# Sums of weight blocks by accumulating DMAs instead of VectorE subtractions, in a hybrid decoder block on one Trainium2 core

## The chip, the cores and the metric

The program runs on one core of one Trainium2 chip. The metric is the device time of one execution in microseconds (us); the figure used is the median of several executions. Engines are called as in the profile: PE (TensorE matmul), PEld (its weight loads), DVE (VectorE), ACT (ScalarE), POOL (GpSimd), SP (SyncE, which here only issues DMAs).

## The reference

One decoder block on x (256 tokens, 1024 channels). A normalised input goes through one input projection w_in; a gated linear recurrence (HGRN2) and a block attention (MoBA) work on parts of it; both branch outputs are projected, each gated by a sigmoid, summed, and projected again; a SwiGLU network follows. What matters here is the gate of the first branch, gates[:, :, 0, :], and where it is used:

```python
h = rmsnorm(x, attn_norm_g[l])
proj = h @ w_in[l]
hq, hf, hi, hg, aq, ak, av, gl = jnp.split(proj, IN_SPLITS, axis=-1)
y_hg = hgrn2_mix(hq, hf, hi, hg, lb_all[l], hg_out_norm_g[l]) @ w_branch_hg[l]
...
y_at = att.transpose(0, 2, 1, 3).reshape(B, S, AT_WIDTH) @ w_branch_attn[l]
gates = jax.nn.sigmoid(gl.reshape(B, S, N_BRANCH, D))
merged = gates[:, :, 0, :] * y_hg + gates[:, :, 1, :] * y_at
```

## The kernel before

Weights are float32 and go through PE as two float32r parts: ACT writes the rounded part (`whi`, line 55), DVE the rest (`wlo`, line 56), and each product is three matmuls (hi by hi, lo by hi, hi by lo). Weights come in pieces of 128x2048 floats (1 MB), loaded by SP into a ring of three buffers `wraw`; `whi` and `wlo` have three buffers each. Every engine works its instructions off in a fixed order.

The first branch's gate is a product of 256 tokens x 1024 channels with 1024 columns of w_in that start at column 7168 (`g0`). It isn't computed straight. Tokens are cut in two halves (0 to 127, 128 to 255), channels in two halves, columns in two halves: a 2x2 by 2x2 block product, done with seven block products instead of eight (a scheme of the Strassen kind). Write Bij for the weight block with channel half i and column half j, each 512x512 and 1 MB. `quarter(i, j, tag)` loads one block (tiles W11, W12, W22, W21 in the code). The scheme needs sums and differences of token blocks (made in `token_sums`, lines 585 to 599, tiles C, Ch, Cl) and of weight blocks. The weight tile W11 takes four contents in turn, and after each of them `halves(W11)` splits it (ACT line 55, DVE line 56) for one block product:

- content 1: B11, product b1 with plain tokens;
- content 2: a difference of B12 and B11 (line 676), product b3 with token sum 0;
- content 3: B22 minus content 2 (line 683), product b2 with token sum 1;
- content 4, held in W21: B21 minus content 3 (line 702), last product b2 with plain tokens.

W12 becomes B22 minus B12 (line 684), for token sum 2. These four subtractions are DVE instructions on 128x2048 floats.

The block products (`product`, line 620, 12 matmuls each) alternate on PE with half column blocks of the attention branch's projection (`step`, lines 657 to 659, 24 matmuls each, weights w_at). The order of PE is: b1 of content 1; transposes `turn` (line 442) of the recurrence's output; step; b3 of content 2; step; b2 of content 3; b1 with B21; step; b2 with W12; step; b3 with B22; b2 of content 4; then the projection w_hg. `then` and `issue_after` pin this order. `put` (lines 446 to 457) turns the transposes into the split tiles oT. In the traces the four W tiles are all called W.

Of the kernel before, what the change touches and what calls it, by code (L numbers as in the profile page):

```python
# [7 lines left out]
F32 = mybir.dt.float32  # L8
F32R = mybir.dt.float32r
U32 = mybir.dt.uint32  # L10
AF = mybir.ActivationFunctionType
OP = mybir.AluOpType
AX = mybir.AxisListType

P = 128
S = 256
# [11 lines left out]
def tile_hgrn2_moba_block(ctx: ExitStack, tc: tile.TileContext, xm, xT, vecs, table, onehot,  # L28
                          w_in, w_hg, w_at, w_out, w_gate, w_up, w_down, out):
    nc = tc.nc  # L30
    const = ctx.enter_context(tc.tile_pool(name="const", bufs=1))
# [6 lines left out]
    def pw(name="pw"):  # L38
        return psum.tile([P, 512], F32, name=name, tag="pw", bufs=4)
# [4 lines left out]
    def pa(name="pa"):  # L44
        return psum.tile([P, 512], F32, name=name, tag="pa", bufs=2)
# [8 lines left out]
    def split(src, hi, lo):  # L54
        high = nc.scalar.copy(hi, src)  # L55
        return high, nc.vector.tensor_sub(lo, src, hi.bitcast(F32))  # L56

    halved = []
# [95 lines left out]
    for kt in range(KT):  # L154
        i = kt % 2
# [17 lines left out]
        else:  # L173
# [3 lines left out]
                                       op0=OP.mult, op1=OP.subtract)  # L177
        nc.scalar.copy(wh[:, i, 512:D], raw[:, i, 512:D])  # L178
        for hs in (slice(0, 512), slice(512, D)):
            low = nc.vector.tensor_sub(wl[:, i, hs], raw[:, i, hs], wh[:, i, hs].bitcast(F32))  # L180
# [15 lines left out]
    for j in range(7):  # L196
        c = 1 << j
# [9 lines left out]
    def rinv(dst, ss, n):  # L207
        nc.vector.tensor_scalar(dst, ss, 1.0 / n, EPS, op0=OP.mult, op1=OP.add)
        nc.scalar.activation(dst, dst, AF.Sqrt)
        nc.vector.reciprocal(dst, dst)  # L210
# [35 lines left out]
        nc.scalar.activation(junk, xtok[:, tb, :], AF.Square, accum_out=ss[:, tb:tb + 1])  # L246
    rx = const.tile([P, 2], F32, name="rx")
    rinv(rx, ss, D)
    def put_tok(dst, ps, half):
        for tb in range(2):  # L250
            nc.scalar.mul(dst[:, tb, half * 512:(half + 1) * 512], ps[tb], rx[:, tb:tb + 1])

    put_tok(V, V0, 0)
    put_tok(V, V1, 1)
    R = const.tile([P, S], F32, name="R")
    spread(R, rx)
# [7 lines left out]
    for half in range(2):  # L264
        ps = F0 if half == 0 else feat_block(w_in, 1024 + half * 512, XT, cut=2 - half)
        for j in range(2):
# [8 lines left out]
            for i in range(2):  # L275
                hh = slice(h + i, h + i + 1)
                nc.vector.tensor_scalar(Fg[:, :, h + i, :], Fg[:, :, h + i, :], lc[:, hh], lb[:, hh],
                                        op0=OP.mult, op1=OP.add)
# [151 lines left out]
    def hgrn_gate(o, ro, sg, banks):  # L430
        for tb in range(2):
            for h in range(H):
                hs = slice(h * P, (h + 1) * P)
                nc.vector.scalar_tensor_tensor(o[:, tb, hs], o[:, tb, hs], ro[:, tb, h:h + 1], sg[:, tb, hs],
                                               op0=OP.mult, op1=OP.mult)
        oT = [big.tile([P, 4, 2, S], F32R, name=f"oT{i}", tag=("T3", "T4")[i]) for i in range(2)]
        for g in range(4):
            bank = banks[g]
            for i in range(2):
                for tb in range(2):  # L440
                    h = 2 * g + i
                    last = nc.tensor.transpose(bank[:, i * S + tb * P:i * S + (tb + 1) * P],
                                               o[:, tb, h * P:(h + 1) * P], ident)

        def put(high, low):
            for g in range(4):
                q = 2 * g % 4
                with tc.issue_after(high.ins):
                    nc.scalar.mul(oT[g // 2][:, q:q + 2, 0, :], banks[g].rearrange("p (h t) -> p h t", h=2), og)
            for g in range(4):  # L450
                q = 2 * g % 4
                with tc.issue_after(low.ins):
                    nc.vector.scalar_tensor_tensor(oT[g // 2][:, q:q + 2, 1, :],
                                                   banks[g].rearrange("p (h t) -> p h t", h=2), og,
                                                   oT[g // 2][:, q:q + 2, 0, :].bitcast(F32),
                                                   op0=OP.mult, op1=OP.subtract)

        return oT, put, last


    def qk_block(tok, sq, c0, half, bank=pw):
        put_tok(tok, tok_block(w_in, c0 + half * 512, XT, bank=bank), half)
        for tb in range(2):
            for h in range(half * 4, half * 4 + 4):
                jk = small.tile([P, P], F32, name="jk")
                nc.scalar.activation(jk, tok[:, tb, h * P:(h + 1) * P], AF.Square, accum_out=sq[:, tb, h:h + 1])
# [119 lines left out]
    def token_sums():  # L586
        F = big.tile([P, 2, 4, S], F32, name="F", tag="T1")
        C = big.tile([P, 4, 4, P], F32, name="C", tag="T3")
        hi = big.tile([P, 4, 4, P], F32R, name="Ch", tag="T5")
        lo = [big.tile([P, 2, 4, P], F32R, name=f"Cl{i}", tag=("T13", "T15")[i]) for i in range(2)]  # L590
        for i in range(2):
            nc.vector.tensor_add(F[:, i], XT[i][:, :, 0, :].bitcast(F32), XT[i][:, :, 1, :].bitcast(F32))
        nc.vector.tensor_add(C[:, 0], F[:, 0, :, P:S], F[:, 1, :, P:S])
        nc.vector.tensor_sub(C[:, 1], C[:, 0], F[:, 0, :, 0:P])
        nc.vector.tensor_sub(C[:, 2], F[:, 0, :, 0:P], F[:, 0, :, P:S])
        nc.vector.tensor_sub(C[:, 3], F[:, 1, :, 0:P], C[:, 1])
        for i in range(2):
            split(C[:, 2 * i:2 * i + 2], hi[:, 2 * i:2 * i + 2], lo[i])
        return [hi[:, c] for c in range(4)], [lo[c // 2][:, c % 2] for c in range(4)]


    g0 = 7168

    def quarter(i, j, tag):
        t = big.tile([P, 4, 512], F32, name=f"W{i}{j}", tag=tag)
        nc.sync.dma_start(t, w_in[i * 512:(i + 1) * 512, g0 + j * 512:g0 + (j + 1) * 512]
                          .rearrange("(k p) c -> p k c", p=P))
        return t

    def halves(raw):  # L610
        hi = wp.tile([P, 4, 512], F32R, name="whi")
        lo = wp.tile([P, 4, 512], F32R, name="wlo")
        halved.append(split(raw, hi, lo))
        return hi, lo
# [9 lines left out]
    def tokens(i, j):  # L624
        return lambda kt, m: XT[j][:, kt, m, i * P:(i + 1) * P]

    def summed(c):
        return lambda kt, m: sums[m][c][:, kt, :]
# [3 lines left out]
    A01 = hgrn_cross()  # L632
    o, ro = hgrn_out(A01)
    sums = token_sums()
    W11 = quarter(0, 0, "T9")
    W12 = quarter(0, 1, "T1")
    branch_gate(1, 1)
    turn_a, b1, turn_h, b3 = pa("turn"), pa("b1"), ph("turn"), ph("b3")
    product(b1, tokens(0, 0), halves(W11), True)
    oT, put_oT, at = hgrn_gate(o, ro, sg, (turn_a, turn_h, pw("turn"), pw("turn")))  # L640

    def then(f, *args):
        with tc.issue_after(at.ins):
            return f(*args)
# [3 lines left out]
    def at_block(half):  # L648
        ps = [pw(), pw()]
        steps = chunks(w_at, half * 512, 512, (4, 4))  # L650

        def step():
            for _ in range(4):
                kt, wh, wl = next(steps)
                for tb in range(2):
                    ts = slice(tb * P, (tb + 1) * P)
                    nc.tensor.matmul(ps[tb], part(aT, kt, 0)[:, ts], wh, start=(kt == 0), stop=False)  # L657
                    nc.tensor.matmul(ps[tb], part(aT, kt, 0)[:, ts], wl, start=False, stop=False)  # L658
                    mm = nc.tensor.matmul(ps[tb], part(aT, kt, 1)[:, ts], wh, start=False, stop=(kt == KT - 1))  # L659
            return mm  # L660

        def out():
            hs = slice(half * 512, (half + 1) * 512)
            for tb in range(2):
                nc.vector.tensor_mul(G[1][:, tb, hs], G[1][:, tb, hs], ps[tb])

        return step, out

    def gq(i, j):
        return G[0][:, i, j * 512:(j + 1) * 512]  # L670

    def sigmoid(i, j, src):
        nc.scalar.activation(gq(i, j), src, AF.Sigmoid, scale=rx[:, i:i + 1])

    nc.scalar.copy(gq(1, 0), b1)
    nc.vector.tensor_sub(W11, W12, W11)
    step0, out0 = at_block(0)
    at = then(step0)
    at = then(product, b3, summed(0), halves(W11), True)
    W22 = quarter(1, 1, "T8")  # L680
    at = then(step0)
    with tc.issue_after(halved[-1][1].ins):
        nc.vector.tensor_sub(W11, W22, W11)
        low = nc.vector.tensor_sub(W12, W22, W12)
    put_oT(halved[-1][0], low)
    b2 = pa("b2")
    at = then(product, b2, summed(1), halves(W11), True)
    W21 = quarter(1, 0, "T2")
    at = then(product, b1, tokens(0, 1), halves(W21), False)
    sigmoid(0, 0, b1)  # L690
    step1, out1 = at_block(1)
    at = then(step1)
# [3 lines left out]
    at = then(product, b2, summed(2), halves(W12), False)  # L696
# [1 line left out]
    nc.vector.tensor_add(gq(1, 1), gq(1, 1), b3)  # L698
    sigmoid(1, 1, gq(1, 1))
    at = then(step1)  # L700
    with tc.issue_after(halved[-1][1].ins):
        nc.vector.tensor_sub(W21, W21, W11)
    out1()
    at = then(product, b3, summed(3), halves(W22), False)
    nc.vector.tensor_add(gq(0, 1), gq(0, 1), b3)
    sigmoid(0, 1, gq(0, 1))
    at = then(product, b2, tokens(1, 1), halves(W21), False)
    nc.vector.tensor_add(gq(1, 0), b2, gq(1, 0))
    sigmoid(1, 0, gq(1, 0))

# [148 lines left out]
```

## Time and profile before

| | before |
|---|---|
| median of 3 runs | 497.64 us (497.56 to 498.19) |
| profiled execution | 498.32 us, its span 496.3 us, so 2.0 us lie around the span |
| PE busy in the span | 490.4 us |
| DVE busy | 362.5 us |
| ACT busy | 290.7 us |
| POOL busy | 20.3 us |
| granted clock of PE | 1.000 |

The span runs from the first to the last instruction. Busy time counts instructions at work, not waits. An engine that is busy nearly all of the span sets the time; what the others do matters where it makes that engine wait.

### The profile page before, as it was taken

How to read it: one execution, taken by the hardware profiler on the slowest of the kernel's cores; microseconds unless marked ns; L12 is line 12 of the kernel's file. 1: busy time of each engine (PE TensorE's matmuls, PEld its weight loads, DVE VectorE, ACT ScalarE, POOL GpSimd, SP SyncE). 2: the span in 40 equal slices, each digit the busy share in tenths (PEclk: the TensorE clock that was granted, in tenths of full speed). 3: DMA queues.
4: the chain of work that ended last, by engine and by line, in shares of the span. 5: the costliest groups of instructions: out<-in, count | busy, mean ns of one | idle time of the engine just before them, and what ended most of it. 6: DMA issues, size and time to landing. Idle time of an engine off the chain costs nothing.

```text
span 496.3 us, 6659 instructions
## 1 busy us (share of the span) xinstructions
PE 490.4 (99%) x2664; PEld 414.6 (84%) x2664; DVE 362.5 (73%) x414; ACT 290.7 (59%) x410; POOL 20.3 (4%) x43
## 2 busy tenths in 40 slices
PE   8999999999999999999999999999999999999997
PEld 6888888888888888988888888888888888888885
DVE  5769999697679948499987767777636746566373
ACT  5877646777748964874564445764545435444350
POOL 0900220000000000000000000000000000000000
PEclk9999999999999999999999999999999999999999
DMA  8977685624544454327338555555565555643522
GB/s 272 395 269 255 222 255 183 233 85 154 188 169 167 145 198 147 109 81 257 129 127 280 183 183 186 182 173 170 174 221 191 177 173 193 219 136 108 188 86 86
DMA packets 43518, 91.20 MB, mean 184 GB/s; under 512 B 1976, under 2 KB 5336, under 8 KB 43488
## 3 DMA queue, kind: packets, MB, share of 16 engines
q1 hardware_dynamic: 42608, 88.12, 52.0%
q0 software_dynamic: 736, 2.65, 1.7%
q8 instruction: 21, 0.34, 0.3%
q14 instruction: 9, 0.07, 0.0%
q10 hardware_dynamic: 144, 0.02, 0.0%
HBM read 89.70 MB, written 1.07 MB: 183 GB/s over the span
## 4 chain that ended last, share of the span: by engine, by line
PE 98%; DMA 1%; SPq 0%; ACT 0%; DVE 0%; issue 0%
PE pw L101 23%; PE pw L100 10%; PE pw L83 10%; PE pw L84 10%; PE pw L85 10%; PE pw L151 4%; PE acc L782 4%; PE acc L781 4%; PE acc L780 4%; PE b L620 4%; PE pw L658 1%; PE pw L657 1%; PE pw L659 1%; PE pw L103 1%; PE ph L369 1%; DMA wraw<-w_in 1%
## 5 line engine op out<-in xcount | busy, mean ns | idle before, releaser
L56 DVE TENSOR_TENSOR wlo<-wraw,whi 128x2048 fp32r<-128x2048 f32 (+1 forms) x77 | 167.6, 2179 | 87.3 <-ACT whi L55 86.8
L55 ACT CAST whi<-wraw 128x2048 fp32r<-128x2048 f32 (+1 forms) x77 | 140.2, 1823 | 98.0 <-PE pw L85 30.9
L101 PE MATMUL pw<-x2T,whi 128*128 128x512 f32 x352 | 121.9, 398 | 0.0
L100 PE MATMUL pw<-x2T,wlo 128*128 128x256 f32 x308 | 86.6, 281 | 0.0
L101 PEld LDWEIGHTS pw<-x2T,whi 128*128 128x128 f32 x352 | 63.6, 188 | 12.5
L100 PEld LDWEIGHTS pw<-x2T,wlo 128*128 128x128 f32 x308 | 58.3, 189 | 1.8
L83 PE MATMUL pw<-whi,XT 128*128 128x512 f32 x144 | 56.9, 395 | 0.0
L84 PE MATMUL pw<-wlo,XT 128*128 128x512 f32 x144 | 56.2, 391 | 0.0
L85 PE MATMUL pw<-whi,XT 128*128 128x512 f32 x144 | 56.2, 391 | 0.0
L101 PE MATMUL pw<-XT,whi 128*128 128x512 f32 x128 | 44.5, 398 | 0.0
L780 PE MATMUL acc<-whi,hT 128*128 128x512 f32 x86 | 33.5, 390 | 0.0
L782 PE MATMUL acc<-whi,hT 128*128 128x512 f32 x86 | 33.5, 390 | 0.0
L781 PE MATMUL acc<-wlo,hT 128*128 128x512 f32 x86 | 33.5, 390 | 0.0
L85 PEld LDWEIGHTS pw<-whi,XT 128*128 128x128 f32 x144 | 27.0, 188 | 5.6
L83 PEld LDWEIGHTS pw<-whi,XT 128*128 128x128 f32 x144 | 27.1, 188 | 5.6
L84 PEld LDWEIGHTS pw<-wlo,XT 128*128 128x128 f32 x144 | 27.1, 188 | 5.5
L100 PE MATMUL pw<-XT,wlo 128*128 128x256 f32 x112 | 31.5, 281 | 0.0
L101 PEld LDWEIGHTS pw<-XT,whi 128*128 128x128 f32 x128 | 23.2, 188 | 4.5
L100 PEld LDWEIGHTS pw<-XT,wlo 128*128 128x128 f32 x112 | 21.2, 189 | 0.7
L781 PEld LDWEIGHTS acc<-wlo,hT 128*128 128x128 f32 x86 | 16.2, 188 | 3.4
L782 PEld LDWEIGHTS acc<-whi,hT 128*128 128x128 f32 x86 | 16.2, 188 | 3.4
L151 PE MATMUL pw<-whi,XT 128*128 128x512 f32 x64 | 17.7, 393 | 1.2 <-ACT whi L178 1.2
(290 smaller groups left out, 821.6 us busy)
## 6 DMA issues: line engine op xcount, KB each, us to landing
wraw<-w_in SPq DMA_DIRECT2D x26, 1024.0 KB, 5.0
wraw<-w_down SPq DMA_DIRECT2D x11, 1024.0 KB, 4.7
wraw<-w_gate SPq DMA_DIRECT2D x10, 1024.0 KB, 5.0
wraw<-w_up SPq DMA_DIRECT2D x10, 1024.0 KB, 5.0
wraw<-w_in SPq DMA_DIRECT2D x10, 512.0 KB, 7.8
W<-w_in SPq DMA_DIRECT2D x4, 1024.0 KB, 5.0
wraw<-w_at SPq DMA_DIRECT2D x4, 1024.0 KB, 4.9
wraw<-w_hg SPq DMA_DIRECT2D x4, 1024.0 KB, 5.7
```

What stands on the lines that cost most here:

```text
L55: high = nc.scalar.copy(hi, src)
L56: return high, nc.vector.tensor_sub(lo, src, hi.bitcast(F32))
L83: nc.tensor.matmul(ps[tb], part(act, kt, 0)[:, ts], wh, start=(kt == 0), stop=False)
L84: nc.tensor.matmul(ps[tb], part(act, kt, 0)[:, ts], wl, start=False, stop=False)
L85: nc.tensor.matmul(ps[tb], part(act, kt, 1)[:, ts], wh, start=False, stop=(kt == KT - 1))
L100: nc.tensor.matmul(ps[ct][:, 0:S], lo[:, i, cs], part(act, kt, 0), start=False, stop=False)
L101: nc.tensor.matmul(ps[ct], hi[:, i, cs], both, start=(kt == 0), stop=(kt == KT - 1))
L151: nc.tensor.matmul(ps[tb], part(XT, kt, am)[:, tb * P:(tb + 1) * P], w[:, i, hs], start=(kt == 0 and am == 0 and w is wh), stop=(kt == KT ...
L620: mm = nc.tensor.matmul(bank, act(kt, m), h[:, kt, :], start=(first and kt == 0 and m == 0 and h is hi), stop=(kt == 3 and m == 1), skip_g ...
L780: nc.tensor.matmul(acc[tb][half], act[:, j, 0, ts], hi[:, i, cs], start=st, stop=False)
L781: nc.tensor.matmul(acc[tb][half], act[:, j, 0, ts], lo[:, i, cs], start=False, stop=False)
L782: nc.tensor.matmul(acc[tb][half], act[:, j, 1, ts], hi[:, i, cs], start=False, stop=en)
```

## The change

The weight sums become plain sums: W11 holds in turn B11, B11+B12, B11+B12+B22 and B11+B12+B22+B21, and W12 holds B12+B22. Each addition is a DMA that POOL issues and that adds a block from HBM into the tile (`accum_op=OP.add`). The signs move into the token sums (two subtractions become `scalar_tensor_tensor` with a factor of -1) and into two sigmoids, which take the scale rn = -rx for columns of half 1. The four DVE subtractions go. B12, B22 and B21 are still loaded into tiles of their own, so the adds read 4 MB more from HBM.

```diff
+    rn = const.tile([P, 2], F32, name="rn")
+    nc.vector.tensor_scalar_mul(rn, rx, -1.0)
...
-        nc.vector.tensor_add(C[:, 0], F[:, 0, :, P:S], F[:, 1, :, P:S])
-        nc.vector.tensor_sub(C[:, 1], C[:, 0], F[:, 0, :, 0:P])
+        nc.vector.tensor_sub(C[:, 0], F[:, 1, :, P:S], F[:, 0, :, P:S])
+        nc.vector.scalar_tensor_tensor(C[:, 1], C[:, 0], -1.0, F[:, 0, :, 0:P], op0=OP.mult, op1=OP.subtract)
...
-        nc.vector.tensor_sub(C[:, 3], F[:, 1, :, 0:P], C[:, 1])
+        nc.vector.scalar_tensor_tensor(C[:, 3], F[:, 1, :, 0:P], -1.0, C[:, 1], op0=OP.mult, op1=OP.subtract)
...
+    def block(i, j):
+        return w_in[i * 512:(i + 1) * 512, g0 + j * 512:g0 + (j + 1) * 512].rearrange("(k p) c -> p k c", p=P)
...
+    def add_quarter(t, i, j):
+        nc.gpsimd.dma_start(t, block(i, j), accum_op=OP.add)
...
-        nc.scalar.activation(gq(i, j), src, AF.Sigmoid, scale=rx[:, i:i + 1])
+        nc.scalar.activation(gq(i, j), src, AF.Sigmoid, scale=(rx, rn)[j][:, i:i + 1])
...
-    nc.vector.tensor_sub(W11, W12, W11)
+    add_quarter(W11, 0, 1)
...
-    with tc.issue_after(halved[-1][1].ins):
-        nc.vector.tensor_sub(W11, W22, W11)
-        low = nc.vector.tensor_sub(W12, W22, W12)
-    put_oT(halved[-1][0], low)
+    add_quarter(W11, 1, 1)
+    add_quarter(W12, 1, 1)
+    put_oT(*halved[-1])
...
     W21 = quarter(1, 0, "T2")
+    add_quarter(W11, 1, 0)
...
-    with tc.issue_after(halved[-1][1].ins):
-        nc.vector.tensor_sub(W21, W21, W11)
...
-    at = then(product, b2, tokens(1, 1), halves(W21), False)
+    at = then(product, b2, tokens(1, 1), halves(W11), False)
```

How the instructions stand now is shown at two places. The first is POOL's queue at its end. Before, it holds one load of x (the tokens again, for the residual sum) behind two copies of the attention bias:

```order
L312 COPY B_577<-Bx 128x1024 [waits DMASW1_49,PE_49]
L312 COPY B_578<-Bx 128x8x128 [waits DMASW3_49]
L714 DMA x_2274<-xm 128x2x1024 [waits DMAHW4_49,DMAHW5_49,DMAHW1_49,DMAHW7_49,DMAHW0_49,DVE_49]
```

Of the change, W_1898 is W11 and W_1900 is W12:

```order
L315 COPY B_579<-Bx 128x1024 [waits DMASW1_49,PE_49]
L315 COPY B_580<-Bx 128x8x128 [waits DMASW3_49]
L616 DMA W_1900<-w_in 128x4x512 [waits DMAHW1_49,DMAHW4_49,DMAHW0_49,DMAHW5_49,DVE_49,DMAHW7_49,PE_49,Activation_49]
L616 DMA W_1898<-w_in 128x4x512 [waits DVE_49]
L616 DMA W_1898<-w_in 128x4x512 [waits DMASW5_49,DVE_49]
L616 DMA W_1898<-w_in 128x4x512 [waits DMASW6_49,DVE_49]
L720 DMA x_2276<-xm 128x2x1024 [waits DMASW4_49,DVE_49]
```

Four adds stand ahead of the load of x: that into W12 first, then the three into W11, each of which waits for DVE (the split of the content before) and for the add before it.

The second place is DVE around the third content of W11. Before (W_1896 is W11, W_1898 W12, W_2071 W22, W_2130 W21):

```order
L434 SCALAR_TENSOR_TENSOR o<-o,ro,sg 128x128 x15
L56 TENSOR_TENSOR wlo<-wraw,whi 128x2048 [waits DMAHW5_49,Activation_49]
L56 TENSOR_TENSOR wlo<-W_1896,whi 128x2048 [waits PE_49,Activation_49]
L56 TENSOR_TENSOR wlo<-wraw,whi 128x2048 [waits DMAHW6_49,PE_49,Activation_49]
L683 TENSOR_TENSOR W_1896<-W_2071,W_1896 128x2048 [waits DMAHW1_49,DVE_49]
L684 TENSOR_TENSOR W_1898<-W_2071,W_1898 128x2048
L453 SCALAR_TENSOR_TENSOR oT_2002<-turn,vec,oT_2002 128x2x256 [waits Activation_49] x2
L453 SCALAR_TENSOR_TENSOR oT_2003<-turn,vec,oT_2003 128x2x256 [waits Activation_49] x2
L56 TENSOR_TENSOR wlo<-W_1896,whi 128x2048 [waits Activation_49]
L56 TENSOR_TENSOR wlo<-W_2130,whi 128x2048 [waits DMAHW3_49,Activation_49]
```

Of the change (W_1898 is W11, W_2132 W21):

```order
L437 SCALAR_TENSOR_TENSOR o<-o,ro,sg 128x128 x15
L56 TENSOR_TENSOR wlo<-wraw,whi 128x2048 [waits DMAHW5_49,Activation_49]
L56 TENSOR_TENSOR wlo<-W_1898,whi 128x2048 [waits DMASW5_49,PE_49,Activation_49]
L56 TENSOR_TENSOR wlo<-wraw,whi 128x2048 [waits DMAHW6_49,PE_49,Activation_49]
L456 SCALAR_TENSOR_TENSOR oT_2004<-turn,vec,oT_2004 128x2x256 [waits Activation_49] x2
L456 SCALAR_TENSOR_TENSOR oT_2005<-turn,vec,oT_2005 128x2x256 [waits Activation_49] x2
L56 TENSOR_TENSOR wlo<-W_1898,whi 128x2048 [waits DMASW6_49,Activation_49]
L56 TENSOR_TENSOR wlo<-W_2132,whi 128x2048 [waits DMAHW3_49,Activation_49]
```

The two subtractions are gone from between the splits, and the splits of W11 wait for a POOL DMA (DMASW5, DMASW6) in their place. The instructions of PE, ACT and SP stand in the same order as before.

## Rows read from the trace of the kernel before

**Rows 1.** Page, busy time: us, share of the span, instructions.
```profile
PE 490.4 (99%) x2664; PEld 414.6 (84%) x2664; DVE 362.5 (73%) x414; ACT 290.7 (59%) x410; POOL 20.3 (4%) x43
```

**Rows 2.** Busy time by stretches of 10 us around the block products.
```profile
core 0: us, PE busy (x) PEld busy (x) DVE busy (x) ACT busy (x) POOL busy (x), PEclk, DMA share, GB/s
205.00:215.00 10.00, 10.00 (x55) 8.64 (x55) 8.87 (x10) 9.25 (x11) 0.00 (x0) 1.00 0.01 2
215.00:225.00 10.00, 10.00 (x54) 8.52 (x53) 10.00 (x19) 8.23 (x10) 0.00 (x0) 1.00 0.46 161
225.00:235.00 10.00, 10.00 (x46) 8.29 (x45) 10.00 (x9) 4.41 (x4) 0.00 (x0) 1.00 0.71 258
```

**Rows 3.** Timeline of PE: start, duration, line, operands of single matmuls.
```profile
227.88 0.39 PE L620 MATMUL b<-whi,Ch 128*128 128x512 f32 x1
228.11 0.39 PE L620 MATMUL b<-wlo,Ch 128*128 128x512 f32 x1
...
236.04 0.39 PE L620 MATMUL b<-whi,Ch 128*128 128x512 f32 x1
236.27 0.39 PE L620 MATMUL b<-wlo,Ch 128*128 128x512 f32 x1
...
257.82 0.39 PE L620 MATMUL b<-whi,XT 128*128 128x512 f32 x1
```

**Rows 4.** Timeline of DVE, splits, subtractions and the gate of o.
```profile
206.67 2.29 DVE L56 TENSOR_TENSOR wlo<-W,whi 128x2048 fp32r<-128x2048 f32 x1 [1.09 <-ACT whi L55]
...
210.07 2.28 DVE L676 TENSOR_TENSOR W<-W,W 128x2048 f32<-128x2048 f32 x1
212.27 0.17 DVE L208 TENSOR_SCALAR ro<-so 128x16 f32<-128x16 f32 x1
...
214.90 4.29 DVE L434 SCALAR_TENSOR_TENSOR o<-o,ro,sg 128x128 f32<-128x128 f32 x16
219.11 2.29 DVE L56 TENSOR_TENSOR wlo<-wraw,whi 128x2048 fp32r<-128x2048 f32 x1
221.31 2.28 DVE L56 TENSOR_TENSOR wlo<-W,whi 128x2048 fp32r<-128x2048 f32 x1
...
225.71 2.29 DVE L683 TENSOR_TENSOR W<-W,W 128x2048 f32<-128x2048 f32 x1
...
230.12 2.72 DVE L453 SCALAR_TENSOR_TENSOR oT<-turn,vec,oT 128x512 fp32r<-128x512 f32 x4
```

**Rows 5.** Timeline of ACT: the casts of W11's second and third content.
```profile
218.74 1.91 ACT L55 CAST whi<-W 128x2048 fp32r<-128x2048 f32 x1
...
228.13 1.91 ACT L55 CAST whi<-W 128x2048 fp32r<-128x2048 f32 x1 [2.54 <-PE pw L659]
```

**Rows 6.** Timeline of SP: issue of 1 MB loads.
```profile
195.00 0.37 SPq L606 DMA_DIRECT2D W<-w_in  x1
198.94 0.37 SPq L66 DMA_DIRECT2D wraw<-w_at  x1
219.22 0.37 SPq L606 DMA_DIRECT2D W<-w_in  x1
221.42 0.37 SPq L66 DMA_DIRECT2D wraw<-w_at  x1
222.62 0.37 SPq L606 DMA_DIRECT2D W<-w_in  x1
225.83 0.37 SPq L66 DMA_DIRECT2D wraw<-w_hg  x1
```

**Rows 7.** Page, DMA issues: count, KB each, median us from issue to landing.
```profile
W<-w_in SPq DMA_DIRECT2D x4, 1024.0 KB, 5.0
...
Bx<-line_d POOLq DMA_DIRECT2D x2, 512.0 KB, 8.0
x<-xm POOLq DMA_DIRECT2D x1, 1024.0 KB, 5.2
```

**Rows 8.** DMA queues from 240 to 252 us: packets, MB, share of 16 engines.
```profile
q1 hardware_dynamic: 975, 1.96, 45.2%
q0 software_dynamic: 272, 1.05, 26.9%
```

**Rows 9.** DMA queue from 225 to 228 us, columns as in rows 8.
```profile
q1 hardware_dynamic: 590, 1.18, 105.2%
```

**Rows 10.** Busy time by stretches of 2 us, columns as in rows 2.
```profile
219.00:221.00 2.00, 2.00 (x12) 1.64 (x11) 2.00 (x2) 1.77 (x2) 0.00 (x0) 1.00 0.31 62
221.00:223.00 2.00, 2.00 (x18) 1.91 (x17) 2.00 (x2) 2.00 (x2) 0.00 (x0) 1.00 0.99 376
229.00:231.00 2.00, 2.00 (x10) 1.67 (x9) 2.00 (x3) 1.19 (x2) 0.00 (x0) 1.00 0.98 364
231.00:233.00 2.00, 2.00 (x10) 1.65 (x10) 2.00 (x4) 1.76 (x1) 0.00 (x0) 1.00 0.44 166
```

More of the change, by code (lines that the diff above doesn't have):

```diff
@@ L602, in tile_hgrn2_moba_block @@
     g0 = 7168
+    def block(i, j):
+        return w_in[i * 512:(i + 1) * 512, g0 + j * 512:g0 + (j + 1) * 512].rearrange("(k p) c -> p k c", p=P)
     def quarter(i, j, tag):
         t = big.tile([P, 4, 512], F32, name=f"W{i}{j}", tag=tag)
-        nc.sync.dma_start(t, w_in[i * 512:(i + 1) * 512, g0 + j * 512:g0 + (j + 1) * 512]
-                          .rearrange("(k p) c -> p k c", p=P))
-        return t
+        nc.sync.dma_start(t, block(i, j))
+        return t
+    def add_quarter(t, i, j):
+        nc.gpsimd.dma_start(t, block(i, j), accum_op=OP.add)
     def halves(raw):
```

## The prediction

> **What bounds the kernel now.** I read the page's busy times first: PE works 490.4 us of a span of 496.3 us [rows 1]. The edit lies between 205 and 262 us, so I asked for that stretch by itself: PE is busy 10.00 of each 10 us there, and DVE too is at 10.00 of 10 from 215 to 235 us [rows 2]. That DVE is full does not make it the limit: the chain that ended last runs through PE alone here, and the wait list of 200 to 262 us has no wait of PE in it. So each microsecond by which an operand misses its matmul is a microsecond at the end, and an operand that comes earlier buys nothing. PE's order is unchanged. The question is only how much time each new sum of weights has between the moment its tile may be written and the matmul that needs it.
>
> The deadlines are starts of matmuls [rows 3]. A product's second matmul is the first to read `wlo`: 228.11 us for content 2 of W11, 236.27 us for content 3; content 4 is needed from 257.82 us. Ahead of that second matmul lie an ACT cast of 1.91 us [rows 5] and a DVE split of 2.28 us [rows 4], 4.2 us together. A sum must therefore be in its tile by 223.9, by about 232.0 and by about 253.8 us.
>
> **What goes and what is added, part by part.**
>
> *Four DVE subtractions go.* At 2.28 us each (three of the four are shown) [rows 4] that is 9.1 us of DVE. PE is worth nothing by it directly, but one consequence counts: without the one at 210.07 us, `ro` and the gate of o that follows (L434) can come 2.1 us earlier, limited by ACT's square root. The gate then ends at about 217.1 instead of 219.2 us, the next split (L56, 219.11 us) is out of the way by 219.4, and the split of content 2 can follow its cast at once: cast 218.74 to 220.65 us [rows 5], split to 222.93 instead of 223.6 us. SP's load of B22, which waits for the gate, moves from 219.22 [rows 6] to about 217.1 us, and the w_at load behind it from 221.42 to 219.4 us; the load of B21 waits for PE and stays at 222.6, w_hg stays at 225.8 us.
>
> *Signs.* The two `scalar_tensor_tensor` in the token sums work on the same 128x512 floats as the subtractions that they replace; four such instructions (L453) take 2.72 us, 0.68 each, and nothing waits for them until content 2. `rn` is one tiny DVE instruction; one on 128x16 takes 0.17 us [rows 4]. The sigmoids only read another scale. Sum: 0, and at most 0.2 us if `rn` had no cover early on.
>
> *Four accumulating DMAs.* The trace has no such transfer. I price one from the nearest, POOL's load of x: 1 MB, 5.2 us from issue to landing [rows 7]. Its packets took 26.9% of 16 engines over 12 us, 3.2 us of the whole set; SP's loads took 45.2% of 12 us for 1.96 MB, 2.9 us for 1.05 MB [rows 8]. So a POOL transfer has about 2.0 us of latency around 3.2 us of work. The lower bound of an add is this: 3.2 us of work. But an add must fetch the old content of the tile too, which a copy doesn't; I count that as one more copy, 6.4 us, and as the upper bound three copies (both fetches and the write apart), 9.6 us. A farther row is the 0.5 MB bias copies at 8.0 us to landing [rows 7], which would make 16 us of 1 MB; they were three at a time in runs of 512 bytes, so I keep it only as the far end. I take 6.4 us: fetching the destination cannot be avoided, and a second pass over the data is the smallest price for it.
>
> The Trainium skill, "Collectives: The Full Stack", section "The bandwidth ceiling: the fold count and why AG ≠ RS ≠ AR", says of a reducing transfer that it isn't slower because adding costs cycles, but because it reads two sources through one ring, and so runs at half the rate of a copy. The row of x alone, taken as the price, would give no stall; the rule's factor of two gives the stall below. No run here shows it yet.
>
> *Are the engines free?* At the first two adds, yes: the DMA share from 205 to 215 us is 0.01 [rows 2]. B12 loaded into W12 is issued at 195.00 us [rows 6] and takes 5.0 us [rows 7], so POOL's first add (into W12) may start at 200.0: about 1.4 us of lead, 6.4 us of work, 1.9 us lost to the rest of the w_at load issued at 198.94 [rows 6], done near 209.7 us. It is needed for a cast at about 239 us: covered by nearly 30 us. The first add into W11 waits for the split that ends at 208.96 us [rows 4]: 208.96 + 2.0 + 6.4 = 217.4 us, before ACT gets to it at 218.74 us. Covered, by 1.4 us.
>
> At the second add into W11, no: SP's four loads hold the engines at 0.98 to 0.99 from 221 us on until after 231 us [rows 10]; from 225 to 228 us they move 1.18 MB in 105% of 3 us, 2.8 us for 1.05 MB [rows 9]. The add may start when content 2 is split, 222.93 us. Its data would start near 224.4 us, when of SP's work, the front of it moved up by 2.1 us, about 4.8 us is left: 2.0 of B21, 2.8 of w_hg. Without that, it would land at 222.93 + 2.0 + 6.4 = 231.3 us, 0.7 us ahead of 232.0. If the two queues halve the engines, the add loses 4.8 us: 236.1 us, 4.1 us late. If they take turns by packet and an add's packet is twice as long as one of SP's, the add gets two thirds: 9.6 us of data, 234.5 us, 2.5 us late. The middle is 3.3 us.
>
> The Trainium skill, "DMA: Bandwidth & Descriptors", section "Issuing engines are not separate DMA queues", speaks against the change: transfers of all issuing engines run on the same 16 DMA engines and interleave, so that POOL's queue brings no bandwidth of its own. By that rule the adds pay the 2.5 to 4.1 us; if POOL's queue ran beside SP's at no loss, they would pay nothing.
>
> *What waits behind it.* ACT stands at the cast of content 3; behind it are the casts of B21 and of the next w_at piece. Each needs 1.9 us on ACT and 2.3 on DVE against 2.72 us of PE for a product, so they keep ahead of PE once it moves; no second stall. The third add, into content 4, starts when content 3 is split (near 239.5 us), takes 8.4 us plus some sharing, 248 to 251 us; its deadline, moved with PE, is 253.8 + 3.3 = 257.1 us. The load of x follows in POOL's queue and is read only near 295 us. W12 and B22 are in long before. PE is full from there to the end, so nothing is won back.
>
> *Sum.* 498.32 us of the profiled execution (span 496.3 and 2.0 around it) + 3.3 = 501.6 us. That execution stands 0.68 us above the median; against it, 497.64 + 3.3 = 500.9 us.
>
> **The rivals.**
>
> *A, forecast:* the second add into W11 is late and PE waits before `wlo` of content 3; +2.5 to +4.1 us, with the doubt on the 6.4 us +1.2 to +5. 500.9 us. Chance 0.50.
>
> *B, the other side: hidden.* If an add costs what a copy does, its 3.2 us even at half rate land at 222.93 + 2.0 + 6.4 = 231.3 us; or the add keeps its 6.4 us because its queue isn't slowed. Either is in time: 497.6 us. The point that decides is 9.1 us from the end of content 2's split to landing. For it: x landed in 5.2 us; the margin that is missing is small. Against: the engines are full just then. Chance 0.31.
>
> *C, dearer adds.* With 9.6 us of work the first add into W11 queues behind that into W12 (data done near 213 us) and lands near 223 us, the split of content 2 ends near 227.2, and the next add lands at 227.2 + 2.0 + 9.6 + 1.0 of sharing = 239.8 us, 7.8 us late: 505.4 us. With the far end of 16 us it would be 13 us. Against it: it takes a price that no row needs. Chance 0.14.
>
> *D, faster,* because DVE, full for 20 us, is relieved. PE had no wait there to lose; a gain would have to come from elsewhere, of at most the 5.9 us that PE isn't busy in the whole span, which lie at its two ends. 496 us. Chance 0.04.
>
> That the adds don't come where the code has them is so: POOL's order has W12's add first. At 6.4 us it costs nothing, at 9.6 us it is part of C. The last 0.01 is for the rest.
>
> **How the numbers follow.** Within 0.2% of before (1.0 us, about what a measurement of this kernel can tell from no change) lie B and the lowest part of A: 0.32. Slower are the rest of A and C: 0.64. Faster is D: 0.04. The forecast is A's 500.9 us; its own range is 498.9 to 502.6 us. The range that holds 8 in 10 takes in B below and C at its 9.6 us above: 497.3 to 505.5 us.
>
> **What would show it.** In the changed kernel's POOL rows: adds issued near 200, 209, 223 and 239 us, with 8 to 9 us to landing for the first two, 11 to 13 for the third. ACT's cast of content 3 then starts near 235 us, released by a DMA, and PE shows one gap, of about 3 us, before `b<-wlo,Ch` of that product and none elsewhere between 205 and 262 us. If the third add lands before 232 us, B holds. If the cast of content 2 too starts after 218.7 us, it is C. The forecast is wrong at its root if an add's packets take about 3.2 us of the 16 engines, or far over 6.4.

## The result and the profile after

The changed kernel takes 504.05 us (503.65 to 504.65, 4 runs) against 497.62 us (497.56 to 498.19): 1.0128 times the time before, 95% interval 1.011 to 1.0145, 6.4 us slower. Its profiled execution took 503.65 us with a span of 501.9 us.

POOL's timeline first: start, duration, and in brackets how long POOL stood idle and what released it.

```profile
200.03 1.33 POOL L616 DMA_DIRECT2D W<-w_in  x1 [131.31 <-ACT G L579]
208.76 1.29 POOL L616 DMA_DIRECT2D W<-w_in  x1 [7.41 <-DVE wlo L56]
222.76 1.26 POOL L616 DMA_DIRECT2D W<-w_in  x1 [12.71 <-DVE wlo L56]
240.03 1.27 POOL L616 DMA_DIRECT2D W<-w_in  x1 [16.00 <-DVE wlo L56]
```

The adds are issued where the prediction put them: W12 at 200, the three into W11 at 209, 223 and 240 us. How much of the 16 engines they took shows in the queue lines (packets, MB, share) of three stretches: 200 to 208.6 us (add into W12, both queues), 208.7 to 217.5 us (first into W11, alone), 222 to 236 us (second into W11, both queues, and the landings of what was issued there). q0 is POOL's queue, q1 that of SP. The last line is of the kernel before, from 218 to 236 us.

```profile
q0 software_dynamic: 528, 1.05, 67.2%
q1 hardware_dynamic: 513, 1.02, 31.2%
...
q0 software_dynamic: 528, 1.05, 70.3%
...
q1 hardware_dynamic: 1350, 2.67, 54.9%
q0 software_dynamic: 528, 1.05, 43.7%
issues: line engine op xcount, KB each, median us to landing
W<-w_in SPq DMA_DIRECT2D x1, 1024.0 KB, 5.7
W<-w_in POOLq DMA_DIRECT2D x1, 1024.0 KB, 12.6
wraw<-w_hg SPq DMA_DIRECT2D x1, 1024.0 KB, 11.3
...
wraw<-w_hg SPq DMA_DIRECT2D x1, 1024.0 KB, 7.1
```

67.2% of 8.6 us, 70.3% of 8.8 us and 43.7% of 14 us are 5.8, 6.2 and 6.1 us of all 16 engines for 1 MB, where the load of x took 3.2 us [rows 8]. The first add into W11 had the engines to itself and landed 8.3 us after issue. The add into W12 landed after 8.6 us: a w_at load went through in the same stretch (1.02 MB), most of it before the add's own packets began to move. The second add into W11, beside two of SP's loads, took 12.6 us, and the w_hg load beside it 11.3 instead of 7.1 us.

How the two queues shared shows in stretches of 1 us: 225 to 226, 228 to 229 and 231 to 232 us of the change, and last 224 to 225 us of the third experiment below, where the loads are kept away.

```profile
q1 hardware_dynamic: 180, 0.37, 104.5%
...
q0 software_dynamic: 88, 0.18, 101.6%
...
q0 software_dynamic: 64, 0.13, 70.4%
q1 hardware_dynamic: 64, 0.13, 39.2%
...
q0 software_dynamic: 16, 0.03, 33.9%
```

Until 226 us the add moves nothing, behind the loads that were issued before it; with these kept away it begins at about 224.6 us. Then it has the engines almost alone, and from 230 us on its packets and those of w_hg go through one for one, 64 and 64, each of the add's taking nearly twice as long.

Who waited for that, in the timelines of ACT, DVE and PE:

```profile
218.24 1.90 ACT L55 CAST whi<-W 128x2048 fp32r<-128x2048 f32 x1
...
235.51 3.70 ACT L55 CAST whi<-W 128x2048 fp32r<-128x2048 f32 x2 [10.42 <-DMA W<-w_in]
```
```profile
225.01 2.72 DVE L456 SCALAR_TENSOR_TENSOR oT<-turn,vec,oT 128x512 fp32r<-128x512 f32 x4
237.44 4.50 DVE L56 TENSOR_TENSOR wlo<-W,whi 128x2048 fp32r<-128x2048 f32 x2 [9.70 <-ACT whi L55]
```
```profile
227.38 0.39 PE L628 MATMUL b<-whi,Ch 128*128 128x512 f32 x1
...
237.46 0.50 PE L628 MATMUL b<-whi,Ch 128*128 128x512 f32 x1 [1.76 <-ACT whi L55]
239.78 0.51 PE L628 MATMUL b<-wlo,Ch 128*128 128x512 f32 x1 [1.82 <-DVE wlo L56]
...
240.94 0.63 PE L628 MATMUL b<-wlo,Ch 128*128 128x512 f32 x1
241.37 0.63 PE L628 MATMUL b<-whi,Cl 128*128 128x512 f32 x1
...
265.84 0.39 PE L83 MATMUL pw<-whi,oT 128*128 128x512 f32 x1
```

ACT casts content 2 on time, at 218.24 us. It had cast content 3 at 228.13 us before [rows 5]; now it stands 10.4 us and starts at 235.51, when the add lands; DVE has its oT work done by 227.7 us and stands 9.7 us behind ACT; PE waits twice, for the first hi and then for the first lo. From 227.38 us (first matmul of content 2) to the lo of content 3 it is 12.40 us, before 236.27 - 227.88 = 8.39 [rows 3]: **4.0 us late**. From there to the first matmul of w_hg it is 26.06 us, before 260.54 - 236.27 = 24.27 us, though PE waits nowhere in it: **1.8 us more**. The end of that stretch in the kernel before:

```profile
260.54 0.39 PE L83 MATMUL pw<-whi,oT 128*128 128x512 f32 x1
```

Busy time by stretches of 1 us of the change (columns as in [rows 2]) says where the 1.8 us go:

```profile
239.00:240.00 1.00, 0.21 (x1) 0.22 (x2) 1.00 (x2) 1.00 (x2) 0.00 (x0) 1.00 0.00 0
240.00:241.00 1.00, 1.00 (x4) 0.76 (x4) 1.00 (x1) 1.00 (x1) 0.97 (x1) 0.57 0.00 0
241.00:242.00 1.00, 1.00 (x4) 0.81 (x3) 1.00 (x2) 0.01 (x1) 0.29 (x1) 0.50 0.06 16
242.00:243.00 1.00, 1.00 (x3) 0.79 (x3) 1.00 (x1) 0.00 (x0) 0.00 (x0) 0.50 0.91 113
243.00:244.00 1.00, 1.00 (x4) 0.74 (x3) 1.00 (x1) 0.00 (x0) 0.00 (x0) 0.72 1.07 188
244.00:245.00 1.00, 1.00 (x6) 0.82 (x5) 1.00 (x3) 0.80 (x1) 0.00 (x0) 1.00 1.11 205
```

PE's granted clock (the number behind POOL's) falls to 0.50, the 1.2 GHz level, right behind the gap, and is back at 2.4 GHz by 244 us; matmuls start 0.43 us apart there (240.94 and 241.37 us) where 0.23 us is usual [rows 3]. So 5.8 us are lost between 227 and 266 us.

The rest is at the ends. The profiled execution of before had come to that point 0.5 us later (227.88 against 227.38 us), so the two spans differ by less, 5.6 us, than the stretch. And the end of the program is some 0.3 us longer (last section).

### The profile page after: what moved, and what is told of

Its sections match the earlier page's. It is cut to its first block, busy times and chain, and to the rows that moved or that the text cites. A ratio compares the mean times of both kernels' runs of the same rounds, so it can differ in the third digit from the quotient of the medians.

```text
span 501.9 us, 6665 instructions
## 1 busy us (share of the span) xinstructions
PE 492.5 (98%) x2664; PEld 415.5 (83%) x2664; DVE 354.3 (71%) x411; ACT 290.8 (58%) x410; POOL 25.6 (5%) x47
## 3 DMA queue, kind: packets, MB, share of 16 engines
HBM read 93.90 MB, written 1.07 MB: 189 GB/s over the span
## 4 chain that ended last, share of the span: by engine, by line
PE 93%; DMA 3%; ACT 1%; DVE 1%; SPq 0%; issue 0%; ACTq 0%
PE pw L101 22%; PE pw L100 10%; PE pw L83 10%; PE pw L84 9%; PE pw L85 9%; PE pw L151 4%; PE acc L786 4%; PE acc L788 4%; PE acc L787 4%; PE b L628 3%; DMA W<-w_in 3%; PE pw L103 1%; PE ph L372 1%; DMA wraw<-w_in 1%; DVE wlo L56 1%; ACT whi L55 1%
## 5 line engine op out<-in xcount | busy, mean ns | idle before, releaser
L101 PEld LDWEIGHTS pw<-x2T,whi 128*128 128x128 f32 x352 | 63.5, 188 | 12.5
L83 PE MATMUL pw<-whi,XT 128*128 128x512 f32 x144 | 56.9, 395 | 0.0
L85 PE MATMUL pw<-whi,XT 128*128 128x512 f32 x144 | 56.2, 390 | 0.0
L56 DVE TENSOR_TENSOR wlo<-W,whi 128x2048 fp32r<-128x2048 f32 x7 | 15.9, 2290 | 14.9 <-ACT whi L55 14.9
L55 ACT CAST whi<-W 128x2048 fp32r<-128x2048 f32 x7 | 13.3, 1908 | 17.4 <-DMA W<-w_in 10.4
```

What stands on the lines that cost most here:

```text
L83: nc.tensor.matmul(ps[tb], part(act, kt, 0)[:, ts], wh, start=(kt == 0), stop=False)
L85: nc.tensor.matmul(ps[tb], part(act, kt, 1)[:, ts], wh, start=False, stop=(kt == KT - 1))
L101: nc.tensor.matmul(ps[ct], hi[:, i, cs], both, start=(kt == 0), stop=(kt == KT - 1))
```

## The experiments

Below, "late" is the time from the first matmul of content 2 to the first `wlo` matmul of content 3, less the 8.39 us of before; "behind" is what the stretch from there to the first w_hg matmul takes above 24.27 us. Both are read from the PE rows of each profiled run, as above. "Third add" is the third that POOL issues, the second into W11; its landing is counted from its issue. Ratios are against runs of the kernel before on the same chip (median 497.83 us beside 1 to 4, 497.86 us beside 5 to 8).

| kernel | time, us | ratio (95%) | third add to landing, us | late, us | behind, us |
|---|---|---|---|---|---|
| the change | 504.05 | 1.0128 (1.011 to 1.0145) | 12.6 | 4.0 | 1.8 |
| 1 copies | 498.40 | 1.0016 (1.0006 to 1.0027) | 10.2 | 1.6 | 0.2 |
| 2 third sum on DVE | 497.93 | 1.0001 (0.9992 to 1.001) | none | 0.0 | 0.0 |
| 3 quiet engines | 498.51 | 1.0013 (1.0004 to 1.0022) | 8.5 | 0.0 | 0.1 |
| 4 filled gap | 503.22 | 1.0104 (1.009 to 1.0118) | 13.7 | 5.1 | 0.2 |
| 5 half quiet | 500.73 | 1.0059 (1.0046 to 1.0071) | 9.3 | 0.7 | 1.6 |
| 6 signs alone | 497.91 | 0.9999 (0.999 to 1.0009) | none | 0.0 | 0.0 |
| 7 the change again | 504.52 | 1.0137 (1.0121 to 1.0153) | 14.0 | 5.3 | 2.2 |
| 8 filled gap again | 502.83 | 1.0102 (1.0089 to 1.0116) | 13.0 | 4.4 | 0.2 |

The theory: one add, the second into W11, lands late, because an add takes twice a copy's work and shares the engines with SP's loads; PE waits, and its clock falls. The rivals: the queue or the crowd alone makes it late, whatever the transfer does; or the signs, the other adds and the 4 MB of extra reads cost part of it.

**1, copies for adds.**
```diff
-        nc.gpsimd.dma_start(t, block(i, j), accum_op=OP.add)
+        nc.gpsimd.dma_start(t, block(i, j))
```


> The four adds become plain copies of the same blocks on the same POOL queue, with the same waits (so the weight blocks are copies, not sums, and the gate's values are others). Theory, the second read of an accumulating transfer is the price: the third transfer takes about 3 us of the 16 engines instead of 5.8, lands 8 to 9 us after its issue instead of 12.6, before 232 us, PE doesn't wait, and the time is 497.6 us within 0.7. Rival, POOL's queue or the crowd of SP's loads alone make it late: it lands 11 to 13 us after its issue and the time stays at 502 to 504 us.

A copy's share is 33.6% of 9.5 us, 3.2 us of the engines, against 5.8 to 6.2 for an add. From 208.5 to 218 us (second copy, alone), and for the third one from 222 to 236 us:

```profile
q0 software_dynamic: 272, 1.05, 33.6%
...
W<-w_in POOLq DMA_DIRECT2D x1, 1024.0 KB, 5.4
...
q0 software_dynamic: 272, 1.05, 19.4%
issues: line engine op xcount, KB each, median us to landing
W<-w_in SPq DMA_DIRECT2D x1, 1024.0 KB, 7.6
W<-w_in POOLq DMA_DIRECT2D x1, 1024.0 KB, 10.2
```
```profile
237.25 0.50 PE L628 MATMUL b<-wlo,Ch 128*128 128x512 f32 x1 [1.46 <-DVE wlo L56]
```

The doubled work is most of the loss: without it 0.6 of 6.4 us are left. But the expectation was too good: the copy took 10.2 us where I expected 8 to 9, and PE still waited 1.5 us in the profiled run. The crowd delays a copy as much as an add: 10.2 us to landing instead of 5.4 alone, where an add took 12.6 instead of 8.3. In the change PE would have read the first lo at 227.38 + 8.39 = 235.77 us, and from the landing to that matmul pass 4.4 us (235.36 to 239.78), so the third add, issued at 222.76 us, has some 8.6 us to land in time. An add alone just fits into that, and a copy in the crowd just doesn't; the big loss needs both.

**2, only the third sum back on DVE.**
```diff
-    add_quarter(W11, 1, 1)
+    with tc.issue_after(halved[-1][1].ins):
+        nc.vector.tensor_add(W11, W11, W22)
```


> Only the third sum of W11's row (B22 into B11+B12) goes back to DVE, as a tensor_add behind the split of the w_at piece; the other three sums stay accumulating DMAs and the signs stay as changed. Theory, that one add is all of the loss: 497.6 us within 0.7, no gap on PE between 205 and 262 us, granted clock 1.00. Rival, the 4 MB of extra reads, the other adds or the signs cost too: 1 us or more above, in proportion.

As the theory had it: no wait of PE between 205 and 268 us, and the time of before. Three adds with 3 MB of extra reads cost nothing that can be measured. They gain nothing either, though DVE has three 2.28 us subtractions less.

**3, quiet engines.** B21 goes behind the add on POOL's queue; the first w_hg load waits until the add has landed.
```diff
-    add_quarter(W11, 1, 1)
+    third = add_quarter(W11, 1, 1)
+    mark = small.tile([P, 1], F32, name="mark")
+    nc.vector.tensor_copy(mark, W11[:, 0, 0:1])
...
-    W21 = quarter(1, 0, "T2")
+    W21 = big.tile([P, 4, 512], F32, name="W21", tag="T2")
+    with tc.issue_after(third.ins):
+        nc.gpsimd.dma_start(W21, block(1, 0))
...
+    hold.append(mark)
...
+        if hold:
+            nc.vector.tensor_copy(raw[:, 0, 0:1], hold.pop())
```


> The adds stay. The load of B21 goes behind the third add on POOL's queue, and the first load of w_hg waits (by a one-column write into its buffer) until that add has landed, so nothing shares the engines with it but the end of the w_at load. Theory, the sharing is the late part: the third add lands 8.5 to 9.5 us after its issue as the first two did, about 231.5 us, PE waits 0 to 0.5 us, 497.5 to 498.7 us. Rival, an add into a tile is slow by itself whatever else runs: 11 to 13 us to landing, 502 to 504 us.

POOL's timeline and ACT's:

```profile
222.75 1.26 POOL L620 DMA_DIRECT2D W<-w_in  x1 [12.71 <-DVE wlo L56]
```
```profile
231.40 1.91 ACT L55 CAST whi<-W 128x2048 fp32r<-128x2048 f32 x1 [6.32 <-DMA W<-w_in]
```

The same add in the same place lands after 8.5 us and ACT starts at 231.4 us. PE comes to this product 0.5 us earlier here than in the profile of before, so the 232.0 us that the prediction allowed are 231.5 us here: in time by a hair, and PE doesn't wait. So the add is late by sharing, not by itself.

**4 and 8, useless work in the gap.**
```diff
+    with tc.issue_after(at.ins):
+        for _ in range(16):
+            nc.tensor.matmul(b2, XT[0][:, 0, 0, 0:P], XT[0][:, 0, :, :].rearrange("p m t -> p (m t)"), start=True, stop=True)
     at = then(product, b2, summed(1), halves(W11), True)
```


> Sixteen useless matmuls of 512 columns (3.6 us) stand on PE ahead of the product that waits; the product's first matmul overwrites what they leave. The third add is as late as before. Theory, the wait itself is about 3.7 us, and the rest of the 6.4 us is TensorE's clock, which falls after PE stood idle: the clock stays at 2.4 GHz (granted 1.00 in all stretches) and the time is 501.0 to 502.2 us. Rival, the clock costs nothing here and the rest is elsewhere: 503.5 to 504.5 us.

> The kernel of the fourth experiment once more (sixteen useless matmuls in the gap), beside the changed kernel. Theory, the clock costs about 1.8 us and the landing of the third add varies by about 1 us from run to run: granted clock 1.00 throughout, and in the median 0.8 to 2.0 us faster than the changed kernel; in the trace, the lateness of the first wlo of content 3 explains the whole difference from before within 0.5 us. Rival, filling the gap gains nothing: the same time within 0.4 us.

PE's timeline in the fourth run, and its busy time by 4 us:

```profile
235.64 3.79 PE L696 MATMUL b<-XT 128*128 128x512 f32 x16
240.92 0.50 PE L628 MATMUL b<-wlo,Ch 128*128 128x512 f32 x1 [1.26 <-DVE wlo L56]
```
```profile
238.00:242.00 4.00, 2.74 (x13) 1.94 (x12) 3.43 (x2) 4.00 (x3) 0.84 (x1) 1.00 0.00 0
242.00:246.00 4.00, 4.00 (x19) 3.31 (x18) 4.00 (x4) 2.06 (x2) 0.43 (x1) 1.00 0.72 110
```

In both profiles the clock stays at 1.00 from 234 to 246 us and "behind" falls from 1.8 to 0.2 us: the second part of the loss is the clock. The fourth run's time, 503.22 us, missed its 501.0 to 502.2; its add landed 1.1 us later than in the first profile of the change, about as much as is missing. Against the first runs of the change it gained 0.8 us in the median, and beside the change on one chip (7 and 8) 1.7 us, inside the 0.8 to 2.0 expected; all eight runs of each taken together, 1.0 us (504.05 and 503.09 us). With four runs a side and times that spread over 2 us, the size of the gain is known only roughly; the traces put the clock's part at 1.8 and 2.2 us.

**5, half quiet:** the third kernel without holding w_hg (the lines with `mark` and `hold` left out).

> As the third experiment, but the first load of w_hg is not held: only the load of B21 stands behind the third add on POOL's queue, so the add shares the engines with one SP load instead of two. Theory, each SP load that shares costs the add time: it lands between the 8.7 us of the third experiment and the 12.6 us of the changed kernel after its issue, 10 to 11.5 us, so 0.5 to 2.5 us late, 499 to 501 us, with TensorE's clock at 2.4 GHz where the gaps are short. Rival, one load is as bad as two: 12 us and more, 502 to 504 us.

The time is inside the range, but not for the reason given. PE's timeline:

```profile
236.56 0.50 PE L628 MATMUL b<-wlo,Ch 128*128 128x512 f32 x1 [0.50 <-DVE wlo L56]
240.69 0.50 PE L628 MATMUL b<-wlo,XT 128*128 128x512 f32 x1 [1.07 <-DVE wlo L56]
```

The add landed after 9.3 us, sooner than the 10 to 11.5 expected: w_hg, issued 2.4 us behind the add, delays it by only 0.8 us against 3. The bigger share of the lateness in the change goes with the load of B21, issued at 222.12 us, just ahead of the add; that fits the add's packets, which there begin only after 226 us. Here, though, B21 itself came late, behind the add and beside w_hg, and the next product, b1, waited for it.

**6, the signs alone,** with the four sums as `tensor_add` on DVE.
```diff
-    add_quarter(W11, 0, 1)
+    nc.vector.tensor_add(W11, W11, W12)
...
-    add_quarter(W11, 1, 1)
-    add_quarter(W12, 1, 1)
-    put_oT(*halved[-1])
+    with tc.issue_after(halved[-1][1].ins):
+        nc.vector.tensor_add(W11, W11, W22)
+        low = nc.vector.tensor_add(W12, W12, W22)
+    put_oT(halved[-1][0], low)
...
-    add_quarter(W11, 1, 0)
...
+    with tc.issue_after(halved[-1][1].ins):
+        nc.vector.tensor_add(W11, W11, W21)
```


> All four sums are made on DVE again, as plain additions, with the signs in the token sums and the two sigmoids as changed: the signs alone. Theory: nothing, 497.8 us within 0.4, the same as before. Rival, the signs cost part of the 6 us: 498.5 us or more.

0.9999, within 0.1%: the signs cost nothing that can be measured.

**7, the change again.**

> The changed kernel once more, beside the next one on the same chip. 503.5 to 504.7 us; third add 12.5 to 13.8 us from issue to landing, PE late by 3.5 to 5 us, and TensorE at 1.2 GHz for 3 to 4 us behind the gap.

The time is inside its range, the rest is not: the add landed after 14.0 us (12.5 to 13.8 expected), PE was 5.3 us late (3.5 to 5), and the clock was at 1.2 GHz for nearly 7 us (3 to 4), because it fell already in the first gap. PE's waits, and busy time by 1 us:

```profile
239.01 0.79 PE L628 MATMUL b<-whi,Ch 128*128 128x512 f32 x1 [3.07 <-ACT whi L55]
241.34 0.79 PE L628 MATMUL b<-wlo,Ch 128*128 128x512 f32 x1 [1.53 <-DVE wlo L56]
```

```profile
238.00:239.00 1.00, 0.00 (x0) 0.00 (x0) 0.01 (x1) 1.00 (x2) 0.00 (x0) 0.95 0.00 0
239.00:240.00 1.00, 0.79 (x1) 0.29 (x1) 1.00 (x1) 1.00 (x1) 0.00 (x0) 0.50 0.00 0
...
245.00:246.00 1.00, 1.00 (x5) 0.78 (x4) 1.00 (x2) 0.00 (x0) 0.00 (x0) 0.63 1.12 205
```

No version beats the kernel before: with PE never waiting in this stretch there, the best that an edit of the sums can do is to equal it, as 2 and 6 do.

## Why the prediction was right, and where its sum fell short

- **PE alone sets the time, DVE's relief is worth nothing.** Right: 2 and 6 take 6.8 us and nothing off DVE and stand at 1.0001 and 0.9999. In the change DVE even stood idle for 9.7 us in one piece.
- **Signs at 0.** Right (6).
- **6.4 us of engine work for an add.** Right in kind, a little high: 5.8 to 6.2 us, a copy by POOL 3.2 us. That agrees with what the Trainium skill, "Collectives: The Full Stack", section "The bandwidth ceiling: the fold count and why AG ≠ RS ≠ AR", states of the collective ReduceScatter: two sources read, half the rate. The add that had the engines to itself landed 8.3 us after issue, where 8.4 was worked out.
- **First add into W11 and the add into W12 covered.** Right: no wait of PE for either, content 2 cast at 218.24 us, and in 2 they stand unchanged at no cost. The add into W12 landed at 208.6 us, where 209.7 was worked out.
- **Second add into W11 late by 2.5 to 4.1 us, 3.3 taken.** Right in mechanism: 4.0 us late in the first profile, 5.3 in the repeat. Taking the sharing away removed it (3), which agrees with the Trainium skill, "DMA: Bandwidth & Descriptors", section "Issuing engines are not separate DMA queues". Halving the engines came nearer in the number, but what the rows show is the other picture, turns by packet: 64 and 64 packets in 1 us, 70.4% and 39.2% of the engines. That picture gave 2.5 us because it, like the other, let the add's data start near 224.4 us; they started after 226 us, behind B21. PE stood twice, before the first hi and before the first lo, where one gap was forecast.
- **Rival B, hidden if an add cost what a copy does.** Its condition was too generous: a copy was put at 8.4 us from issue to landing (231.3 us) and took 10.2 us (232.8 us), and PE was 1.6 us late in that run (1); in the median it was only 0.6 us slower than before.
- **The term that was missing.** "Each microsecond by which an operand misses its matmul is a microsecond at the end" is where the sum failed. Each late microsecond was paid once, but the gap also cost 1.8 us of clock (2.2 in 7), shown by 4 and 8. 4.0 late, 1.8 of clock and some 0.3 at the end are 6.1 in the one profile, where 3.3 was forecast and 6.4 measured in the medians.
- **The range held partly by luck.** The forecast's own range ended at 502.6 us; 504.05 us lies inside 505.5 only because rival C, dearer adds, was taken in above. C is not what happened: an add took 5.8 to 6.2 us of work, not 9.6, and the cast of content 2 was on time. The time between came from a longer wait and from the clock, which no rival had.
- **Two slips without effect.** [rows 4] show two of the four subtractions, not three; and the 13 us for the far end leave out the queueing behind the add into W12 that C counts.

## What to carry to other kernels

Before work moves from an engine to a DMA, look at what the DMA engines do in just that window: a transfer that takes 8.5 us in a quiet stretch (3) took 12.6 to 14.0 us in one where another queue held all 16 engines. What was issued just before it counted more here than what came behind (5). An accumulating DMA of this shape is to be priced as nearly two copies, and one in place stands in a chain (split, add, cast, split) in which each step waits for the one before. Where PE is the bound, a wait of this length must be priced with the slow clock behind it, and a gap that could not be closed was cheaper filled with useless matmuls, here by 0.8 and 1.7 us.

## What the hardware showed that I had not expected

- **A gap in two pieces slowed PE too.** In the first profile PE was idle for 1.76 us, ran one matmul, was idle for 1.82 us, and then ran at 1.2 GHz from about 240.1 to 243.5 us. In the repeat (7) the clock fell near the end of the first gap, of 3.07 us. Single gaps of 1.46 us (1) and 1.26 us behind the filling (4), and gaps of 0.50 and 1.07 us some 4 us apart (5), left the granted clock at 1.00.
- **The landing of a crowded add varies, by its last packets.** The same program's third add landed after 12.6 and 14.0 us in two profiles; filled, after 13.7 and 13.0. In the repeat of the change (7) only a few of its 528 packets were still under way late: 4 from 235 to 236 us and 3 from 236 to 237 us, in 4.4% and 2.3% of the 16 engines' time. In the first profile the last one fell just behind 235 us. What held them is open. In both pairs the profile with the later landing has the longer time; the runs of the change spread from 503.65 to 505.89 us, and the other runs left no trace.
- **The end of the program was longer in the kernels with more POOL transfers.** From the end of the last DVE instruction to the end of the span it is 3.1 us before and in 6, 3.4 to 3.5 us in 2 and in the change (three and four more POOL transfers), and 3.7 us in 3 (five more). Why is open. It may be most of the 0.7 us by which 3, where PE doesn't wait, is slower than before.
